# One address distance between weights and x in each product, 22 distances in the feed-forward pairs

## The chip, the core and the metric

The kernel runs on one core of a Trainium2 chip. The metric is the device time of one execution in microseconds, the median of several runs. Five engines work side by side and meet through semaphores: TensorE (PE, with its weight loads as PEld) multiplies, VectorE (DVE), ScalarE (ACT) and GpSimd (POOL) do everything elementwise, SyncE (SP) issues the DMAs that bring weights from HBM. Operands lie in SBUF, 128 partitions side by side; an address below is the byte offset within a partition. Products are accumulated in PSUM.

## What is computed

Two layers of a sequence model over 256 tokens behind 16 learned ones (272 rows of 1024 features). A layer has three mixers (retention, a gated linear recurrence, differential attention), whose inputs all come from one large projection, and a convolutional feed-forward part:

```python
def mixer(hn, w_in, w_branch, w_out, lb, lam_p, subln_g, lambda_init, valid, pos):
    proj = (hn @ w_in).astype(F32)
    ...
    y_b = jnp.einsum('blnc,ncd->blnd', branches, w_branch.astype(F32))
    gates = jax.nn.sigmoid(mg.reshape(b, l, N_BRANCH, D_MODEL))
    y = jnp.sum(gates * y_b, axis=2)
    return y.astype(hn.dtype) @ w_out

def conv_ffn(hn, w_ffn_in, conv_w, conv_b, w_ffn_out, valid):
    u = jnp.where(valid[None, :, None], hn @ w_ffn_in, 0.0)
    ...
    gate, val = jnp.split(c, 2, axis=-1)
    return (jax.nn.silu(gate) * val) @ w_ffn_out
```

with `h = h + mixer(rms_norm(h))` and `h = h + conv_ffn(rms_norm(h))` in each layer and a last norm. Nearly all arithmetic is in the five kinds of weight products (`w_in`, `w_branch`, `w_out`, `w_ffn_in`, `w_ffn_out`), all in float32.

## The kernel before

Activations lie transposed: features on the partitions, the 272 tokens along the row. Weights stream from HBM in **tiles** of 128 x 128, eight tiles to a **chunk** (512 KB). A chunk lands in `wraw`; ScalarE rounds it to a high part `whi` and VectorE subtracts to get the low part `wlo`. Each operand has such a high and a low part too. So every tile is three matmuls (lines 868 to 870): high weights by high x, high weights by low x, low weights by high x. In the profile the three lines give the beat of TensorE's stream, one beat of three for each tile.

The products are written in **pairs** of output tiles, named by matrix: `hq`, `hf` and so on to `m2` (the 52 pairs of `w_in`, table `BASE`), `b0` to `b2`, `wo`, `fi` (22 pairs, the feed-forward input) and `fo` (4 pairs, the feed-forward output). `ORDER` (line 58) lists them, `_turns` (line 87) the tiles of each pair: for the k tiles of the contraction in turn, the two outputs f. A pair of `w_in` or `fi` has 16 tiles (8 k tiles by 2), a pair of `fo` 44. In pair 3 of `fo` of layer 0 all k come first for one output, then for the other.

In the last layer only the tokens from `T0` = 14 on are needed by most products ("short" ones, 258 words instead of 272); those listed in `FULL` still take all 272. `fo` of the last layer is turned round (weights moving, 512 words, lines 1378 to 1380).

**Places.** The x of the projections and of `fi` lies in six tiles `xs` (line 725): high and low parts of k tiles 0 to 3 and 4 to 7, and a second set for 0 to 3. Each holds four k tiles of 272 words (1088 bytes, which is 64 more than a multiple of 256). `_places` (line 125) gives each weight tile its place in `whi` and `wlo`: it starts at a wanted offset modulo `LINE` = 256 bytes, and adds 64 bytes for every k tile (modulo four), so that within a pair the distance from x to the weights stays the same. In the program as it is allocated the tiles of x begin on a multiple of 256 bytes and all weight buffers 64 bytes behind one. That makes a distance of 64 bytes for full products and of 104 for short ones (96 + 64, less the 56 bytes of `T0`). Products whose operand lies in a **slot** (`b0` to `b2`, `wo`, `fo`) get 64 more, since the slots begin at 64; they have the same distances of 64 and 104. Where the wanted place is `None` (pair 3 of `fo` in layer 0, and `fo` in the last layer) the tiles lie back to back, 512 bytes each.

`_runs` (line 150) merges tiles of a chunk at equal steps, so that one instruction of ScalarE and one of VectorE write a chunk with its gaps.

Slots are 14 buffers of 4 x 272 words (`SLOTS`, line 38) that are used in rotation for heads, attention, operands of later products and the like. The order of all instructions is set before the run by `_Plan.order` from estimated costs and due times, with the number of buffers of each kind as a limit; engines then wait for each other by semaphores only. SP holds one queue: the loads of the weights and of a few constants, in that planned order.

Of the kernel before, what the change touches and what calls it, by code (L numbers as in the profile page):

```python
# [12 lines left out]
F32R = mybir.dt.float32r  # L13
# [6 lines left out]
P = 128  # L20
# [3 lines left out]
T = META + SEQ  # L24
D = 1024
KD = D // P
# [8 lines left out]
TAIL = T - 2 * P  # L35
BANK = 512
CHUNK_TILES = 8
SLOTS = 14
LEAD = 6.0
MARGIN = 12.0  # L40
EARLY = 12.0
# [6 lines left out]
BASE = {"rq": 0, "rk": 4, "rv": 8, "rg": 16, "hq": 24, "hf": 32, "hi": 40, "hg": 48,  # L48
        "dq": 56, "dk": 64, "dv": 72, "m0": 80, "m1": 88, "m2": 96}
# [37 lines left out]
def _turns(li):  # L87

    pairs = [x for x in ORDER if x[0][0] not in MARKS]
    if li == DEPTH - 1:
        pairs = [x for x in pairs if x[0] != "fo"]
    groups = [[x] for x in pairs]
    if li == 0:
        groups[:2] = [pairs[:2]]
    turned = [[x] for n in (BASE, ("fi",)) for x in [x for x in pairs if x[0] in n][DEFER - 1 : DEFER]]
    out = []
    for group in groups:  # L100
        if group == [("fo", 3)]:
            out.append([("fo", 3, k, f) for f in range(2) for k in range(FK)])
        else:
            nk = _ktiles(group[0][0])
            out.append([x + (k, f) for k in range(nk // 2) for x in group for f in range(2)])
            out[-1] += [x + (k, f) for x in group for k in range(nk // 2, nk) for f in range(2)]
            if group in turned:
                out[-1] = out[-1][nk:] + out[-1][:nk]
    if li == DEPTH - 1:
        out.append([("fo", j, k, f) for k in range(FK) for j in range(KD // 2) for f in range(2)])  # L110
    return out
# [5 lines left out]
LINE = 256  # L117
APART = (0, 96)
BLOCK = 64
ROOM = CHUNK_TILES * P + 2 * LINE // 4  # L120
T0 = META - 2
FULL = ("rk", "rv", "hf", "hi", "dk", "dv")


def _places(depth=DEPTH):

    wants = []
    for li in range(depth):  # L130
        for name, j, k, _ in sum(_turns(li), []):
            if name == "fo" and (li == DEPTH - 1 or j == 3):
                wants.append(None)
                continue
            short = li == DEPTH - 1 and name not in FULL
            wants.append(APART[short] + BLOCK * (name[0] == "b" or name in ("wo", "fo")) + 64 * (k % 4))
    out = []
    for c in range(0, len(wants), CHUNK_TILES):
        at, places = 0, []
        for want in wants[c : c + CHUNK_TILES]:  # L140
            if want is not None:
                at += (want // 4 - at) % (LINE // 4)
            places.append(at)
            at += P
        assert at <= ROOM
        out.append(places)
    return out
# [410 lines left out]
class _Weights:  # L558
# [3 lines left out]
    def __init__(self, plan, pool, w, act, dve, sp):  # L562
        self.plan, self.pool, self.w = plan, pool, w
        self.act, self.dve, self.sp = act, dve, sp
        self.used = 0
        self.places = _places()
# [37 lines left out]
def build(tc, a, depth=DEPTH, probe=None):  # L604
    with ExitStack() as ctx:
        plan = _Plan(tc)
        _trace(ctx, tc, plan, a, depth, probe or {})
        plan.issue()
    return plan


def _trace(ctx, tc, plan, a, depth, probe):
# [9 lines left out]
    wp = ctx.enter_context(tc.tile_pool(name="wp", bufs=3))  # L622
    sp = ctx.enter_context(tc.tile_pool(name="sp", bufs=SLOTS))
    gp = ctx.enter_context(tc.tile_pool(name="gp", bufs=3))
# [7 lines left out]
    def new(pool_, shape, dt, tag, bufs, name):  # L632
        serial[0] += 1
        return plan.tile(pool_, shape, dt, tag, bufs, f"{name}_{serial[0]}")

    def fixed(shape, name, dt=F32):
        return new(cp, shape, dt, name, 1, name)

    def slot(name, dt=F32):
        return new(sp, [P, 4 * T], dt, "slot", SLOTS, name)  # L640

# [80 lines left out]
    fmap = fixed([P, DEPTH], "fmap")  # L722
    fixed([P, KD], "step")

    xs = [[fixed([P, KD // 2, T], f"x{n}{i}", F32R) for n in "hl"] for i in range(3)]

    def x_tile(k, folded):
        return tuple(t[:, k % 4, :] for t in xs[1 if k >= 4 else 2 if folded else 0])
# [116 lines left out]
    def products(xs, name, j, t0=0):  # L845

        if name in BASE or name == "fi":
            norm.next()
        if ahead:
            return ahead.pop()  # L850
        tiles = turns.pop(0)
        main = lambda: new(mp, [P, 2, 512], F32, "main", 2, "main")[:, :, t0:T]
        ps = {i: main() for i in sorted({x[1] for x in tiles})}
        to = {x: ps[x[0]][:, x[1], :] for x in {x[1::2] for x in tiles}}
        if (name, j) == ("fo", 3):

            to[j, 1] = main()[:, 1, :]
        cost = 3 * ((T - t0) / 2400 + 0.003)
        left = dict.fromkeys(to, _ktiles(name))
        for _, i, k, f in tiles:  # L860
            hi, lo = (x[:, t0:] for x in xs(k))
            begun = left[i, f] < _ktiles(name)
            left[i, f] -= 1
            plan.key = clock[0]
            wh, wl = weights.next()

            def run(o=to[i, f], wh=wh, wl=wl, hi=hi, lo=lo, first=not begun, last=left[i, f] == 0):
                nc.tensor.matmul(o, wh, hi, start=first, stop=False)  # L868
                nc.tensor.matmul(o, wh, lo, start=False, stop=False)  # L869
                nc.tensor.matmul(o, wl, hi, start=False, stop=last)  # L870

            plan.main.append(plan.add("pe", run, cost, [to[i, f]], [wh, wl, hi, lo]))
            clock[0] += cost
        plan.key = clock[0] - 1.0
        if (name, j) == ("fo", 3):
            return [to[j, f] for f in range(2)]
        ahead.extend(ps[i] for i in ps if i != j)
        return ps[j]
# [64 lines left out]
    for li in range(depth):  # L943
# [458 lines left out]
        for name, j in ORDER:  # L1402
# [18 lines left out]
            elif name[0] == "*":  # L1421
                plan.key = clock[0] - MARGIN
                n = name[1:]
# [10 lines left out]
            if name in BASE:  # L1434
                lo = 0 if name in FULL else t0
                ps = products(lambda k: x_tile(k, norm.folded), name, j, lo)
# [30 lines left out]
                elif name in ("hi", "dv"):  # L1467
                    n = name[0] + "v"
# [109 lines left out]
```

## Time and profile before

| | |
|---|---|
| median of three runs | 1329.39 us (1329.1 to 1330.91) |
| span of the profiled execution, first to last instruction | 1327.6 us |
| difference, around the span | 1.8 us |
| matmuls in the three lines of the weight products | 9168 |
| DMA | 219.07 MB, 165 GB/s in the mean |

The profile shows one execution. Its page gives each engine's busy share, and the views of the trace give groups of instructions by line, waits, and instructions in order of time. In the view by line a row reads: line, engine, operation, output<-inputs, count; then the shortest, median and longest duration in ns and the start of the first and of the last one in us. Matmuls overlap each other in the records, so a matmul's duration is no measure of the pace; the distance from start to start is.

The waits of the whole program by the waits view, longest first (who waited, for whom, total us, times, longest):

```profile
POOL tails L553 <- ACT vsrc L553: 369.7, 23, 57.2
POOL y L553 <- ACT rstd L553: 316.7, 4, 188.3
DVE wlo L553 <- ACT whi L553: 199.8, 175, 4.7
ACT whi L553 <- PE main L869: 162.2, 134, 3.1
```

These are waits of engines that have time to spare: POOL has little to do, ScalarE waits for a weight buffer that TensorE gives back, and VectorE for ScalarE's cast.

### The profile page before, as it was taken

To read this page: it belongs to the slowest core of one execution; us is meant where nothing else is said; L and a number is where in the kernel's file an instruction comes from. 1 tells how busy PE (TensorE), PEld (TensorE's weight loads), DVE (VectorE), ACT (ScalarE), POOL (GpSimd) and SP (SyncE) were. 2 spreads that over 40 slices of the span, in tenths; PEclk is the share of its full clock that TensorE was granted. 3 is DMA by queue.
4 is the path that set the end of the run, shared out by engine and by line. 5 is a ranking of instruction groups with operands and counts; after the bars stand their busy time and mean duration, and the time that the engine had idled before them with its cause. 6 is when DMAs were issued, how large, how long until landed. Compare 5 with 4: busy or idle time off the path is not lost.

```text
span 1327.6 us, 28926 instructions
## 1 busy us (share of the span) xinstructions
PE 1317.0 (99%) x11862; PEld 1288.8 (97%) x11862; DVE 962.7 (73%) x1630; ACT 816.7 (62%) x1374; POOL 83.6 (6%) x161
## 2 busy tenths in 40 slices
PE   9999999999999999999999999999999999999998
PEld 9999999999999999999999999999999999999986
DVE  7675777697586789886574757776985867898753
ACT  6747454756676567666456474557565775767643
POOL 5000000001010020000030000000011100200000
PEclk9999999999999999999999999999999999999999
DMA  7644543443534545555555445444445446465653
GB/s 272 195 146 155 170 150 128 143 143 129 188 131 158 177 157 176 187 168 186 175 175 181 155 159 161 160 140 143 143 149 175 142 162 199 135 208 189 201 182 109
DMA packets 60755, 219.07 MB, mean 165 GB/s; under 512 B 6864, under 2 KB 6992, under 8 KB 60624
## 3 DMA queue, kind: packets, MB, share of 16 engines
q1 hardware_dynamic: 60336, 216.71, 49.1%
q8 instruction: 93, 1.52, 0.5%
q10 hardware_dynamic: 288, 0.52, 0.1%
q14 instruction: 38, 0.31, 0.1%
HBM read 216.16 MB, written 1.05 MB: 164 GB/s over the span
## 4 chain that ended last, share of the span: by engine, by line
PE 95%; DVE 3%; issue 1%; DMA 0%; ACT 0%; SPq 0%; DVEq 0%
PE main L868 28%; PE main L870 27%; PE main L869 27%; PE fo L1380 2%; PE fo L1378 2%; PE fo L1379 2%; PE lev L1059 1%; DVE two_b L553 1%; PE ds L1243 1%; PE ms L553 1%; PE do L553 1%; DVE wlo L553 1%; PE ro L553 1%; PE ho L553 1%; PE vt L553 1%
## 5 line engine op out<-in xcount | busy, mean ns | idle before, releaser
L868 PE MATMUL main<-xh,whi 128*128 128x272 f32 (+1 forms) x2368 | 693.2, 293 | 0.2 <-ACT whi L553 0.2
L870 PE MATMUL main<-xh,wlo 128*128 128x272 f32 (+1 forms) x2368 | 680.5, 287 | 0.8 <-DVE wlo L553 0.7
L869 PE MATMUL main<-xl,whi 128*128 128x272 f32 (+1 forms) x2368 | 671.6, 284 | 1.6 <-DVE xl L553 1.5
L553 DVE TENSOR_TENSOR wlo<-wraw,whi 128x1024 fp32r<-128x1024 f32 (+1 forms) x408 | 497.1, 1223 | 200.9 <-ACT whi L553 199.8
L553 ACT ACTIVATE whi<-wraw 128x1024 fp32r<-128x1024 f32 (+1 forms) x408 | 426.6, 1048 | 229.5 <-PE main L869 162.2
L869 PEld LDWEIGHTS main<-xl,whi 128*128 128x128 f32 x2368 | 448.9, 190 | 2.5 <-DVE xl L553 2.1
L868 PEld LDWEIGHTS main<-xh,whi 128*128 128x128 f32 x2368 | 445.6, 188 | 2.5 <-issue 0.7
L870 PEld LDWEIGHTS main<-xh,wlo 128*128 128x128 f32 x2368 | 444.6, 188 | 2.2 <-DVE wlo L553 2.1
L553 DVE SCALAR_TENSOR_TENSOR two_b<-main,small,two_b 128x256 f32<-128x256 f32 (+2 forms) x144 | 65.3, 488 | 29.1 <-ACT two_b L553 27.4
L553 POOL TENSOR_TENSOR y<-h,rstd 128x272 f32<-128x272 f32 x32 | 34.6, 1114 | 316.7 <-ACT rstd L553 316.7
L553 ACT ACTIVATE two_b<-main,small 128x272 f32<-128x272 f32 (+1 forms) x72 | 37.3, 567 | 26.8 <-PE main L870 26.6
L870 PE MATMUL main<-ghi,wlo 128*128 128x272 f32 x176 | 51.0, 290 | 0.0
L868 PE MATMUL main<-ghi,whi 128*128 128x272 f32 x176 | 50.9, 289 | 0.0
L869 PE MATMUL main<-glo,whi 128*128 128x272 f32 x176 | 50.2, 285 | 0.0
L553 ACT ACTIVATE vsrc<-main 128x544 f32<-128x544 f32 x24 | 15.0, 626 | 39.4 <-PE main L870 39.2
L868 PE MATMUL main<-b0hi,whi 128*128 128x272 f32 (+1 forms) x128 | 38.1, 298 | 0.0
L868 PE MATMUL main<-b1hi,whi 128*128 128x272 f32 (+1 forms) x128 | 38.1, 298 | 0.0
L870 PE MATMUL main<-yhi,wlo 128*128 128x272 f32 (+1 forms) x128 | 36.7, 286 | 0.0
L870 PE MATMUL main<-b2hi,wlo 128*128 128x272 f32 (+1 forms) x128 | 36.6, 286 | 0.0
L870 PE MATMUL main<-b1hi,wlo 128*128 128x272 f32 (+1 forms) x128 | 36.6, 286 | 0.0
L870 PE MATMUL main<-b0hi,wlo 128*128 128x272 f32 (+1 forms) x128 | 36.6, 286 | 0.0
L868 PE MATMUL main<-yhi,whi 128*128 128x272 f32 (+1 forms) x128 | 36.5, 285 | 0.0
(244 smaller groups left out, 1936.4 us busy)
## 6 DMA issues: line engine op xcount, KB each, us to landing
wraw<-in_w SPq DMA_DIRECT2D x402, 512.0 KB, 3.4
h<-in_h SPq DMA_DIRECT2D x4, 272.0 KB, 5.2
dec<-in_dec SPq DMA_DIRECT2D x2, 544.0 KB, 5.4
wraw<-in_w SPq DMA_DIRECT2D x4, 256.0 KB, 4.6
const<-in_const SPq DMA_DIRECT2D x1, 937.0 KB, 6.1
gain<-in_gl SPq DMA_DIRECT2D x1, 512.0 KB, 6.1
out<-y ACTq DMA_DIRECT2D x2, 256.0 KB, 2.8
out<-y SPq DMA_DIRECT2D x2, 256.0 KB, 2.7
```

What stands on the lines that cost most here:

```text
L553: self.plan.add(self.name, lambda: f(*args, **kw), cost, outs, ins, args[2] if method == "activation" else None)
L868: nc.tensor.matmul(o, wh, hi, start=first, stop=False)
L869: nc.tensor.matmul(o, wh, lo, start=False, stop=False)
L870: nc.tensor.matmul(o, wl, hi, start=False, stop=last)
L1059: nc.tensor.matmul(o, keys, x, start=True, stop=True)
L1243: nc.tensor.matmul(ss[m][:, at : at + nk], q[half, hd, q0 : q0 + P], k[half, hd, :nk], start=True, stop=True)
L1378: nc.tensor.matmul(o, gh, wh, start=False, stop=False)
L1379: nc.tensor.matmul(o, gl, wh, start=False, stop=False)
L1380: nc.tensor.matmul(o, gh, wl, start=False, stop=end)
```

## The change

```diff
-SLOTS = 14
+SLOTS = 13
...
+SPREAD = [16 * i for i in range(16)] + [8 + 40 * i for i in range(6)]
+WIDE = 320
...
             short = li == DEPTH - 1 and name not in FULL
+            if name in BASE or name == "fi":
+                wants.append((SPREAD[j] + 4 * T0 * short if name == "fi" else APART[short]) % LINE)
+                continue
             wants.append(APART[short] + BLOCK * (name[0] == "b" or name in ("wo", "fo")) + 64 * (k % 4))
...
-    xs = [[fixed([P, KD // 2, T], f"x{n}{i}", F32R) for n in "hl"] for i in range(3)]
+    xs = [[fixed([P, KD // 2, WIDE], f"x{n}{i}", F32R)[:, :, :T] for n in "hl"] for i in range(3)]
```

- Each k tile of x takes 320 words (1280 bytes, five times 256) instead of 272, of which the same 272 are used. All k tiles of x so begin at the same offset modulo 256.
- The weights of the 52 pairs of `w_in` are all put at `APART`, without the 64 bytes for each k tile. Their distance from x is 64 for full and 104 for short products, as before; what goes is that the offset of both moves with k.
- The weights of `fi` pair j are put at `SPREAD[j]` (with 56 bytes for the short ones of the last layer, to make up for `T0`): sixteen multiples of 16, then 8, 48, 88, 128, 168, 208. With the 64 bytes at which the weight buffers begin the distances are 64 + `SPREAD[j]` modulo 256, the same list in both layers.
- The wider x takes 4608 bytes more of each partition; one slot of 4352 bytes is given up. The addresses of slots and weight buffers stay 64 past a multiple of 256.

The built program has the same instructions in the same order on all five engines. What differs in them, beside addresses, is the shape of the casts: where tiles stood at steps of 64 bytes, a chunk was written as four runs of 256 words; now one run of 1024 does it. On ScalarE, in the middle of the feed-forward input of layer 0, before (`whi` is the rounded chunk, `two_b` the convolution, `ghi` the high part of the gated product):

```order
L553 ACTIVATE whi_1031<-wraw_1030 128x4x256
L553 ACTIVATE ghi_1015<-two_b_1017 128x272
L553 ACTIVATE two_b_1025<-main_1018,small_76 128x272 x2
L553 ACTIVATE whi_1036<-wraw_1035 128x4x256
L553 ACTIVATE two_b_1025<-two_b_1025 128x272
L553 ACTIVATE whi_1039<-wraw_1038 128x4x256
```

and with the change:

```order
L558 ACTIVATE whi_1031<-wraw_1030 128x1024
L558 ACTIVATE ghi_1015<-two_b_1017 128x272
L558 ACTIVATE two_b_1025<-main_1018,small_76 128x272 x2
L558 ACTIVATE whi_1036<-wraw_1035 128x1024
L558 ACTIVATE two_b_1025<-two_b_1025 128x272
L558 ACTIVATE whi_1039<-wraw_1038 128x1024
```

Nothing has moved; the cast of each chunk is one run. VectorE's subtraction changes in the same way. Since a slot now comes round after 13 uses, a dozen of the waits on semaphores differ (nine on POOL, two on VectorE, one on SP).

## Prediction

> **What bounds the kernel now.** I read the page's first two parts, then the waits of TensorE (PE), then single stretches by line and in order of time. The first rows of the page:
>
> ```profile
> span 1327.6 us, 28926 instructions
> PE 1317.0 (99%) x11862; PEld 1288.8 (97%) x11862; DVE 962.7 (73%) x1630; ACT 816.7 (62%) x1374; POOL 83.6 (6%) x161
> PEclk9999999999999999999999999999999999999999
> ```
>
> PE has work in 99% of the span and the granted clock never falls. Everything that PE waited for by the waits view is small; the two longest rows are
>
> ```profile
> PE main L869 <- DVE xl L553: 1.5, 1, 1.5
> PE warm L553 <- POOL ones_d L553: 1.0, 1, 1.0
> ```
>
> So no wait sets the time; the pace does at which one matmul follows another. Over fourteen feed-forward pairs of layer 0 (8 to 21), over a stretch of thirteen pairs of layer 1, and over the last branch product of layer 1, the instructions of line 868 (the first of the three matmuls of every weight tile) read
>
> ```profile
> L868 PE MATMUL main<-xh,whi x224: 287/288/289, 525.4 to 608.8; 128*128 128x272 f32 x112
> L868 PE MATMUL main<-xh,whi x208: 278/283/284, 1178.0 to 1252.4; 128*128 128x258 f32 x104
> L868 PE MATMUL main<-b2hi,whi x64: 278/284/287, 1084.1 to 1106.5; 128*128 128x258 f32 x64
> ```
>
> First start to last start over the count less one is the time of a tile (three matmuls): 83.4 / 223 = 374.0 ns with 272 words, 74.4 / 207 = 359.4 ns with 258 words, and 22.4 / 63 = 355.6 ns for the same 258 words in the branch product. The last two have the same address distance (104 bytes) and differ by 1%: a distance alone does not fix a pace; how the stream came into step counts too.
>
> Why a distance could matter is seen in order of time:
>
> ```profile
> 150.07 0.29 PE L868 MATMUL main<-xh,whi 128*128 128x272 f32 x1
> 150.08 0.19 PEld L869 LDWEIGHTS main<-xl,whi 128*128 128x128 f32 x1
> 150.20 0.28 PE L869 MATMUL main<-xl,whi 128*128 128x272 f32 x1
> 150.21 0.19 PEld L870 LDWEIGHTS main<-xh,wlo 128*128 128x128 f32 x1
> ```
>
> The load for the next matmul starts 0.01 us after the current matmul does: weights and x are read from SBUF at the same moment, each time with the same offset between the two addresses.
>
> **What a distance is worth.** One place of the trace shows it with all else alike. In layer 0, feed-forward output pairs 0 to 2 have weights at 64 bytes from their operand; pair 3 has its tiles back to back, so that its distance goes through 0, 64, 128 and 192. Same width, same order of three matmuls:
>
> ```profile
> L868 PE MATMUL main<-ghi,whi x132: 286/289/290, 609.2 to 658.2; 128*128 128x272 f32 x132
> L868 PE MATMUL main<-ghi,whi x28: 285/289/292, 658.6 to 668.8; 128*128 128x272 f32 x28
> ```
>
> 49.0 / 131 = 374.0 ns against 10.2 / 27 = 377.8 ns: 3.8 ns more a tile, 1%. The first four tiles of pair 3 have distances 128, 64, 0, 192:
>
> ```profile
> 658.57 0.29 PE L868 MATMUL main<-ghi,whi 128*128 128x272 f32 x1
> ...
> 658.95 0.29 PE L868 MATMUL main<-ghi,whi 128*128 128x272 f32 x1
> ...
> 659.32 0.29 PE L868 MATMUL main<-ghi,whi 128*128 128x272 f32 x1
> 659.45 0.29 PE L869 MATMUL main<-glo,whi 128*128 128x272 f32 x1
> 659.58 0.29 PE L870 MATMUL main<-ghi,wlo 128*128 128x272 f32 x1
> 659.70 0.29 PE L868 MATMUL main<-ghi,whi 128*128 128x272 f32 x1
> ```
>
> 0.38, 0.37 and 0.38 us: 64 is the quickest of the three, and the whole spread is some 3%. Single starts there lie 0.12 to 0.13 us apart.
>
> A rule of the Trainium skill speaks against any effect: "TensorE: Matmul & The Clock Gate", section "Step-by-step: what each phase is for", gives TensorE two independent SBUF read ports, so that loading the next weights takes no read bandwidth from the running matmul. By it all distances cost alike and every term below would be 0, which is the last of the rivals. The two rows of line 868 above disagree, by 1%.
>
> **The change part by part.** *Feed-forward input pairs.* Two layers of 22 pairs of 16 tiles, 352 tiles a layer. x now starts every k tile on a 256-byte boundary, the weights of pair j lie 64 + SPREAD[j] behind it (the 64 is where the weight buffers begin), so 64 gives way to all multiples of 16 and a few of 8. In layer 0 I take the mean of pair 3's four distances for the mean over the 22: +3.8 x 352 = +1.3 us. In layer 1 the distance given up is 104 at 359.4 ns a tile; no row there has another distance, so I take the same +3.8, again +1.3 us. Ends for each layer: below, every tile as the quickest rows (0.37 us in layer 0, 355.6 ns in layer 1), about -1.4 us; above, each matmul at the slowest printed step, 0.13 us, 390 ns a tile, +16 x 352 = +5.6 us in layer 0 and taken alike in layer 1. Eighteen of the 22 places have never run here, hence the wide upper end; I choose near the measured four since every step seen lies within 0.13 us.
>
> *All products of x (52 pairs a layer).* Before, x moved 64 bytes with every k and the weights with it, so the load that crosses to the next k stood 64 bytes further off for one matmul in six; now it does not. Two tiles in turn show it in both widths:
>
> ```profile
> 540.35 0.29 PE L868 MATMUL main<-xh,whi 128*128 128x272 f32 x1
> ...
> 540.72 0.29 PE L868 MATMUL main<-xh,whi 128*128 128x272 f32 x1
> ...
> 541.10 0.29 PE L868 MATMUL main<-xh,whi 128*128 128x272 f32 x1
> ```
> ```profile
> 1094.08 0.28 PE L868 MATMUL main<-b2hi,whi 128*128 128x258 f32 x1
> ...
> 1094.44 0.28 PE L868 MATMUL main<-b2hi,whi 128*128 128x258 f32 x1
> ...
> 1094.79 0.28 PE L868 MATMUL main<-b2hi,whi 128*128 128x258 f32 x1
> ```
>
> 0.37 then 0.38; 0.36 then 0.35. The mixer's pairs keep their 64 and 104, so this is all that changes for them: 74 pairs of 272 words (1184 tiles) and 30 of 258 (480 tiles). Ends: all tiles like the shorter (370 and 350 ns) -4 x 1184 - 9.4 x 480 = -9.2 us; all like the longer (380 and 360 ns) +6 x 1184 + 0.6 x 480 = +7.4 us. Which it is the trace cannot say, for a longer tile may only return what the one before gained. I take 0 for the wide ones, since 374.0 lies midway, and for the narrow ones the step from 359.4 to 355.6, -3.8 x 480 = -1.8 us, halved because much of the mixer runs between other PE work: -0.9 us.
>
> *Casts.* ScalarE and VectorE now write each chunk of eight tiles as one run instead of four. Rows for the two forms, from the feed-forward stretch and from the contiguous chunks of the end:
>
> ```profile
> L553 DVE TENSOR_TENSOR wlo<-wraw,whi 128x1024 fp32r<-128x1024 f32 x30 | 36.5, 1218 | 0.7 <-ACT whi L553 0.7
> L553 DVE TENSOR_TENSOR wlo<-wraw,whi 128x1024 fp32r<-128x1024 f32 x20 | 24.5, 1225 | 25.1 <-ACT whi L553 25.1
> ```
>
> 1218 and 1225 ns: no difference, and PE waited for nothing in the first of these stretches. 0 us.
>
> *13 slots.* The order on all five engines stays; a dozen waits change. The two new ones on VectorE, before a write of dq, are for a POOL copy made 105 us earlier, and the load of dec, which stands in SP's queue ahead of weight loads, now waits for a memset of hq, 100 us earlier:
>
> ```profile
> 837.67 0.35 POOL L553 COPY tw<-rk 128x128 f32<-128x128 f32 x1
> 942.62 0.68 DVE L553 TENSOR_TENSOR dq<-main,const 128x516 f32<-128x516 f32 x1
> 748.94 0.15 POOL L553 MEMSET hq<- 128x56 f32 x1
> L553 SPq DMA_DIRECT2D dec<-in_dec x2: 383/404/424, 184.8 to 849.2; - x2
> ```
>
> 0 us. If such a cover were gone, the VectorE work behind dq and the weight loads behind dec would stop, and PE with them; 100 us of slack makes that remote.
>
> Sum: 1.3 + 1.3 - 0.9 = +1.7 us on the profiled span, 1329.3 us. The span lies 1.8 us under the median of the runs (1329.39), so the time is 1329.4 + 1.7 = **1331.1 us**.
>
> **The rivals.** *Costly distances.* The untried places, most of them not multiples of 64, collide at nearly every read, and one pair of two runs at 0.13 us a matmul. For: 0 and 128 already cost more than 64, and in layer 1 the weights come to addresses that are 8 past a multiple of 16, where none was. Against: no four-distance mean is far off. Price: 352 tiles (half of both layers) x 16 = 5.6, the other half at +3.8 is 1.3, less 0.9: +6.0 us, 1335.4. It decides from a mean of 383 ns a tile in layer 0.
>
> The page "SBUF — State Buffer", section "Specifications (TRN2)" of the Trainium skill gives SBUF 16-byte lines and a penalty for each access that crosses to a new one; a weight row that begins 8 bytes into a line touches 33 lines for 32. What that costs no row here shows for weights.
>
> *The even stream is quicker (the other side).* Without the jump of 64 the x products fall into the shorter step, 371 ns for the wide and 353 for the narrow tiles. For: alternate tiles of both streams already have it. Against: pair 3's one tile of 64 without a jump gave 0.37 as well, and its neighbours took the gain back. Price: -3 x 1184 = -3.6, -6.4 x 480 = -3.1, with +2.6 for the feed-forward pairs: -4.1 us, 1325.3. It decides from 372 ns a tile in the wide mixer pairs.
>
> *Distance does nothing* outside pair 3, whose back-to-back tiles are slow for another reason: all terms 0, 1329.4.
>
> **How the numbers follow.** Forecast 0.41, costly distances 0.36, quicker stream 0.18, nothing 0.05. About 0.2% (2.7 us) is what a measurement of this kernel can tell from no change; the forecast and nothing lie inside it, the other two outside: faster 0.18, same 0.46, slower 0.36. The range goes from 1325 (the quicker stream) to 1338 (costly distances with some pairs worse than half at 0.13); it leaves out the far ends of -12 and +18 us.
>
> **What would show it.** In the changed profile: the 22 feed-forward pairs of layer 0, 16 tiles each, should no longer read alike but spread between 370 and 385 ns a tile, mean near 378, with the pair at 64 still near 374; layer 1 near 363. The mixer's wide tiles should stay at 374. PE's waits should stay at a few us, and the branch, wo and fo products unchanged. The forecast is wrong if single pairs exceed 390 ns, if the mixer's tiles move by more than 2 ns, or if a wait of PE's of some us stands where there was none.

## The result, and the profile after

The changed kernel takes 1326.36 us (median of 11 runs, 1325.87 to 1327.05) against 1329.39 us before (11 runs on the same chip, 1328.23 to 1330.91): ratio 0.9975, 95% interval 0.9967 to 0.9984. The forecast was 1331.1 us. The time lies inside the stated range and just outside the 0.2% band, on the faster side. The rival that "the even stream is quicker" had 1325.3 us.

The page of the changed kernel, first lines:

```profile
span 1324.6 us, 28929 instructions
PE 1314.0 (99%) x11862; PEld 1285.7 (97%) x11862; DVE 962.4 (73%) x1630; ACT 816.4 (62%) x1374; POOL 83.2 (6%) x161
```

The span fell by 3.0 us and PE's busy time by the same 3.0 us, while the other engines did the same work. The waits of PE in the changed kernel, the two longest:

```profile
PE main L874 <- DVE xl L558: 1.3, 1, 1.3
PE warm L558 <- POOL ones_d L558: 1.0, 1, 1.0
```

All that PE waited for in this view adds up to 4.1 us in both traces, so the gain is no wait that went: the pace changed. The view by line gives it, as in the prediction: first to last start over the count less one. The first matmul of each tile (now line 873) in six undisturbed wide pairs of the mixer, in fi pairs 8 to 21 of layer 0 (from within pair 8), and in fi pairs 8 to 20 of layer 1; after them the last branch product of layer 1, which the change does not touch. The first row shows the same 96 tiles of the mixer in the kernel before:

```profile
L868 PE MATMUL main<-xh,whi x96: 287/288/289, 37.9 to 73.5; 128*128 128x272 f32 x96
L873 PE MATMUL main<-xh,whi x96: 285/286/288, 38.4 to 73.5; 128*128 128x272 f32 x96
L873 PE MATMUL main<-xh,whi x214: 284/288/295, 526.9 to 607.2; 128*128 128x272 f32 x107
L873 PE MATMUL main<-xh,whi x211: 277/282/287, 1173.8 to 1249.3; 128*128 128x258 f32 x106
L873 PE MATMUL main<-b2hi,whi x64: 278/283/289, 1080.6 to 1103.2; 128*128 128x258 f32 x64
```

35.1 / 95 = 370 ns for the mixer's wide tiles (35.6 / 95 = 374.7 before; 374.0 in hg pairs 0 to 3 by the starts in ns), 80.3 / 213 = 377.0 for the feed-forward tiles of layer 0 (374.0 before), 75.5 / 210 = 359.5 for those of layer 1 (359.4 before). The branch product moved from 355.6 to 22.6 / 63 = 358.7 with the same addresses modulo 256 and the same code.

Where the 3 us went, from the start of the first matmul of each pair in the two traces:

| stretch | before us | after us | difference |
|---|---|---|---|
| up to the first product | 6.1 | 5.6 | -0.5 |
| 52 wide mixer pairs, layer 0 | 360.0 | 358.2 | -1.8 |
| 22 wide mixer pairs, layer 1 | 150.9 | 150.0 | -0.9 |
| 30 narrow mixer pairs, layer 1 | 199.7 | 198.6 | -1.1 |
| 22 feed-forward input pairs, layer 0 | 133.4 | 134.1 | +0.7 |
| the same, layer 1 (pairs 0 to 20) | 123.0 | 123.0 | +0.1 |
| branch, wo and fo products | 279.7 | 280.1 | +0.4 |

The feed-forward pairs lost a little, the mixer gained more. The first row hardly belongs to the change: in the runs below, it lies anywhere between 5.6 and 6.9 us. Each of the 22 distances, in ns a tile (three times the mean from start to start within the pair; intervals over 145 ns, which are interruptions, left out):

| distance | 0 | 16 | 32 | 48 | 64 | 72 | 80 | 96 | 112 | 128 | 144 |
|---|---|---|---|---|---|---|---|---|---|---|---|
| layer 0 | 376 | 375 | 380 | 380 | 370 | 371 | 380 | 371 | 380 | 380 | 371 |
| layer 1 | 360 | 360 | 360 | 360 | 361 | 360 | 353 | 360 | 361, 360 | 357, then 420 | 363 |

| distance | 152 | 160 | 176 | 192 | 208 | 224 | 232 | 240 |
|---|---|---|---|---|---|---|---|---|
| layer 0 | 383 | 376 | 376 | 380 | 377 | 377 | 374 | 375 |
| layer 1 | 360 | 350 | 363 | 360, 359 | 355 | 360 | 356 | 360 |

Two pairs each have 16, 112 and 192; they agree to 1 ns. The means are 376.6 and 360.1 ns. The highest of the wide tiles is 383 ns: none comes near the 390 that the prediction's upper end allowed. In the narrow pair at 128 the pace changed at an interruption half way, from 357 ns a tile to 2.1 / 5 = 420 ns, without any wait after it:

```profile
L873 PE MATMUL main<-xh,whi x6: 306/306/306, 1155.1 to 1157.2; 128*128 128x258 f32 x6
```

### The profile page after: what moved, and what is told of

Same layout as the page of the kernel before. It is cut to its first block, busy times and chain, and to the rows that moved or that the text cites. A ratio compares the mean times of both kernels' runs of the same rounds, so it can differ in the third digit from the quotient of the medians.

```text
span 1324.6 us, 28929 instructions
## 1 busy us (share of the span) xinstructions
PE 1314.0 (99%) x11862; PEld 1285.7 (97%) x11862; DVE 962.4 (73%) x1630; ACT 816.4 (62%) x1374; POOL 83.2 (6%) x161
## 4 chain that ended last, share of the span: by engine, by line
PE 95%; DVE 3%; ACT 1%; issue 0%; DMA 0%; SPq 0%; DVEq 0%
PE main L873 28%; PE main L875 27%; PE main L874 27%; PE fo L1383 2%; PE fo L1385 2%; PE fo L1384 2%; PE lev L1064 1%; DVE two_b L558 1%; PE ds L1248 1%; PE ms L558 1%; PE do L558 1%; PE ro L558 1%; PE ho L558 1%; PE vt L558 1%; DVE wlo L558 1%; PE s L558 0%
## 5 line engine op out<-in xcount | busy, mean ns | idle before, releaser
L873 PE MATMUL main<-b2hi,whi 128*128 128x272 f32 (+1 forms) x128 | 36.5, 285 | 0.0
```

## The experiments

Theory: TensorE's stream is quicker when every weight load stands at the same offset from the x being read, and in the mixer the change does just that; the 22 distances give part of it back. Rivals: the spread itself, the slots, or the 256-byte boundary on which x now begins. All times below are beside runs of the kernel before on the same chip.

**One distance for all products of x.**

```diff
 # changed kernel
-                wants.append((SPREAD[j] + 4 * T0 * short if name == "fi" else APART[short]) % LINE)
+                wants.append(APART[short])
```

> The changed kernel with the feed-forward pairs at the mixer's distances, 64 and 104, in place of the 22. Theory (the steady offset gains, the 22 distances give part of it back): the feed-forward tiles fall to the mixer's pace of the changed kernel, 370 ns in layer 0 and 353.5 ns in layer 1, that is about 2.4 and 2.0 us less: 1322.0 us. Rival (the 22 distances are themselves the gain, or cost nothing): 1326.4 us or more.

Measured: 1324.64 us (6 runs, 1322.46 to 1325.26), ratio to before 0.9969 (0.9956 to 0.9981). Feed-forward tiles in both layers of this kernel:

```profile
L873 PE MATMUL main<-xh,whi x217: 285/285/288, 524.9 to 604.8; 128*128 128x272 f32 x109
L873 PE MATMUL main<-xh,whi x207: 278/278/278, 1171.9 to 1244.7; 128*128 128x258 f32 x104
```

79.9 / 216 = 369.9 ns and 72.8 / 206 = 353.4 ns, as the theory had it. The profiled run took 1322.46 us, the others up to 2.8 us more; the repetition below shows why.

The casts change their form wherever the step goes, so they are a rival for this gain. The same trace answers it, because the casts run ahead of PE. While wo pairs 2 and 3 of layer 0 run, whose weights still step, the chunks that are cast from 464.0 us on are those of `fi`, each in one run. While fi pairs 20 and 21 run, which do not step, the chunks from 596.4 us on are those of `fo`, each in four:

```profile
L873 PE MATMUL main<-yhi,whi x32: 287/288/289, 460.9 to 472.5; 128*128 128x272 f32 x32
L873 PE MATMUL main<-xh,whi x32: 285/286/288, 593.3 to 604.8; 128*128 128x272 f32 x32
```

11.6 / 31 = 374 ns and 11.5 / 31 = 371 ns: each stream keeps its own pace whatever casts run beside it.

**13 slots alone.**

```diff
 # kernel before
-SLOTS = 14
+SLOTS = 13
```

> The kernel before with 13 slots and nothing else. Theory: 1329.4 us, the wide feed-forward tiles at 374 ns. Rival (the moved slots and waits give the gain): 1326.4 us.

Measured: 1329.32 us, ratio 1.0001 (0.9992 to 1.0009). The slots and the dozen changed waits do nothing.

**The 22 distances alone, with the step of 64 bytes.**

```diff
 # kernel before
             short = li == DEPTH - 1 and name not in FULL
+            if name == "fi":
+                wants.append((SPREAD[j] + 4 * T0 * short + 64 * (k % 4)) % LINE)
+                continue
```

> The kernel before (x at 272 words, weights moving 64 bytes with k) with the 22 distances for the feed-forward pairs and nothing else. Theory: the mixer stays at 374 and 359 ns a tile; the feed-forward pairs of layer 0 spread and are slower in the mean by 1 to 4 ns a tile: 1329.5 to 1331.5 us. Rival (spreading the distances gains by itself): under 1328 us.

Measured: 1330.32 us, ratio 1.0012 (1.0003 to 1.0021). The feed-forward tiles of layer 0:

```profile
L872 PE MATMUL main<-xh,whi x226: 282/287/299, 524.7 to 609.4; 128*128 128x272 f32 x113
```

84.7 / 225 = 376.4 ns, 2.4 more than with one distance and the same step: the spread by itself loses. The mixer stayed as before (360.1 us for its wide pairs of layer 0).

Set beside the changed kernel, which has the same 22 distances without the step, this run shows something more. The stretch quoted gave 377.0 ns there, and over all 22 pairs of layer 0 the means are 376.3 ns with the step and 376.6 without. At 64 and 96 bytes the pair with the step is slower (374 against 370 ns, 376 against 371), at 80 and 112 it is quicker (376 against 380 ns, 377 against 380). So a step is no loss as such: without one, a distance runs at a pace of its own, good or bad, and 64 is one of the good ones.

**x 64 bytes past the boundary.**

```diff
 # changed kernel, one distance
-                wants.append(APART[short])
+                wants.append((APART[short] + 64) % LINE)
...
-    xs = [[fixed([P, KD // 2, WIDE], f"x{n}{i}", F32R)[:, :, :T] for n in "hl"] for i in range(3)]
+    xs = [[fixed([P, KD // 2, WIDE], f"x{n}{i}", F32R)[:, :, 16 : 16 + T] for n in "hl"] for i in range(3)]
```

> One distance for all products of x and no step with k, as in the kernel with one distance, but x begins 64 bytes past a 256-byte boundary and the weights move with it. Theory (only the offset between weights and x counts, and that it is steady): same as the kernel with one distance, 1322.0 us, 370 ns a wide tile. Rival (it is the boundary on which every k tile of x begins): wide tiles back at 374 ns, narrow at 359 ns, 1329 us.

Measured: 1325.69 us (9 runs, 1323.4 to 1326.71), ratio 0.9974 (0.9964 to 0.9983). Layer 0, then layer 1:

```profile
L873 PE MATMUL main<-xh,whi x216: 285/286/288, 525.1 to 604.6; 128*128 128x272 f32 x108
L873 PE MATMUL main<-xh,whi x207: 282/285/285, 1171.9 to 1246.7; 128*128 128x258 f32 x104
```

79.5 / 215 = 369.8 ns: for the wide tiles the boundary has no part in it. The narrow ones gave 74.8 / 206 = 363.1 ns, which neither theory had named: slower than with the step of 64 bytes (359.4), at the same distance of 104 that had just run at 353.4. This miss led to the next run.

**One distance once more.** The kernel of the first experiment again, on another chip.

> The kernel with one distance once more, on another occasion. Theory (the narrow stream has two rhythms at the same addresses, 353.4 and 363.3 ns a tile, and which one it falls into after an interruption can differ between executions): wide tiles at 370 as before; feed-forward of layer 1 at one of the two values, times between 1322 and 1326 us. Rival (the addresses alone set the rhythm): 353.4 ns again.

Measured: 1325.19 us (5 runs, 1322.82 to 1326.78), ratio 0.9962 (0.995 to 0.9975). In its profiled execution, fi pairs 1 to 4 of layer 1 (up to an interruption within pair 4) and fi pairs 8 to 20:

```profile
L873 PE MATMUL main<-xh,whi x50: 278/278/278, 1133.9 to 1151.2; 128*128 128x258 f32 x50
L873 PE MATMUL main<-xh,whi x213: 282/285/285, 1171.8 to 1248.8; 128*128 128x258 f32 x107
```

17.3 / 49 = 353 ns, then 77.0 / 212 = 363.2 ns: the same code, addresses and distance, 3% apart within one execution, and in the first profile of this kernel the second stretch ran at 353.4. Even the recorded duration of one matmul tells the two apart (278 against 285 ns). So the narrow stream at distance 104 has two rhythms, and it changes over at an interruption, here in pair 4. Over fi pairs 5 to 21 of layer 1 (272 tiles) the difference of 10 ns is 2.7 us, the size of the scatter between the runs of this kernel.

The kernel before, whose narrow stream steps, has two paces at 104 as well: by the method of the table, fi pairs 2 and 3 of layer 1 ran at 354.2 ns and pairs 6 to 20 at 359.0 in its one trace. So for the narrow tiles no step against a step is one pair of paces against another (353 and 363 against 354 and 359), and what they gained in the changed kernel (353 ns in hg pairs 0 to 3, 359 before) can't be put down to the missing step alone.

**The step at other sizes.** Three kernels keep 64 and 104 within a tile and let x and the weights step by another amount, so that the load that crosses to the next k stands elsewhere.

```diff
 # step 128
-WIDE = 320
+WIDE = 288
...
-                wants.append((SPREAD[j] + 4 * T0 * short if name == "fi" else APART[short]) % LINE)
+                wants.append((APART[short] + 128 * (k % 2)) % LINE)
```
```diff
 # step 80
+WIDE = 276
...
+                wants.append((APART[short] + 80 * (k % 4)) % LINE)
...
+    xs = [[fixed([P, 1152], f"x{n}{i}", F32R)[:, : KD // 2 * WIDE].rearrange("p (a t) -> p a t", t=WIDE)[:, :, :T] for n in "hl"] for i in range(3)]
```
```diff
 # step -64
-SLOTS = 13
+SLOTS = 12
...
-ROOM = CHUNK_TILES * P + 2 * LINE // 4
+ROOM = CHUNK_TILES * P + 3 * LINE // 4
...
+WIDE = 304
...
+                wants.append((APART[short] - 64 * (k % 4)) % LINE)
```

> x in k tiles of 288 words, so that the weights step by 128 bytes with k; distances 64 and 104 within a tile, 192 and 232 on the load that crosses to the next k, instead of 128 and 168 before. Theory (the load at the other offset costs, and what it costs is the pace of that offset): the wide tiles in pairs, about 373 to 374 ns in the mean, since 192 and 128 ran alike in layer 0 of the changed kernel: 1328 to 1330 us. Rival (any step is harmless, it was 128 and 168 alone that cost): 370 ns, 1324.6 us.

> x steps by 80 bytes with k and the weights with it, so that two crossing loads of three stand at 144 instead of 128 (the third, from k tile 3 to 4, at 80). In the changed kernel pairs of one distance ran at 371 ns a tile at 144, 380 at 80 and 128. Theory A (each load costs what its own offset costs, one load in six is a crossing one): wide feed-forward tiles of layer 0 at 370 to 371.5 ns. Theory B (any step between tiles breaks the quick rhythm, whatever the offset): 373 to 374 ns, as with 128 and 192.

> x steps back by 64 bytes with k and the weights with it (12 slots, 256 bytes more in each weight buffer); crossing loads stand at offset 0, where a pair of one distance ran at 376 ns a tile in the changed kernel. Theory A (own offset of each load): 371 ns for the wide feed-forward tiles of layer 0. Theory B (any step breaks the rhythm): 373 to 374 ns.

Measured: step 128, 1330.46 us, ratio 1.0009 (1.0000 to 1.0018); the other two were run once each (1335.54 and 1328.47 us beside 1329.99 before; in the first, two breaks of 3.5 us together inside the recurrence's small matmuls, of no cause that the profile shows, so that only its pace is used). Feed-forward tiles of layer 0 for steps of 128, 80 and -64:

```profile
L873 PE MATMUL main<-xh,whi x223: 286/287/291, 524.9 to 607.8; 128*128 128x272 f32 x112
```
```profile
L873 PE MATMUL main<-xh,whi x224: 283/287/291, 524.9 to 607.9; 128*128 128x272 f32 x112
```
```profile
L873 PE MATMUL main<-xh,whi x223: 287/288/290, 525.0 to 607.7; 128*128 128x272 f32 x112
```

82.9 / 222 = 373.4, 83.0 / 223 = 372.2 and 82.7 / 222 = 372.5 ns, beside 374.0 with the step of 64 and 369.9 without one. Theory A, a sum over the offsets of the single loads, gives 370 + 3 / 6 of the difference per matmul: 371.6, 370.6 and 371. (With the step of 80, three crossing loads of four stand at 144 and the fourth at 80, not two of three as the expectation counts.) All three are above it by 1.5 to 2 ns. Theory B (373 to 374) is nearer, though two of the three fall half a ns or more below it. At the distance of 64 any of these steps costs 2 to 4 ns a tile; its size adds little. The time with the step of 128 lies above the 1330 us of its theory because the narrow tiles, which the theory had left out, went to 365 ns a tile in fi pairs 6 to 20 of layer 1.

**A step after every tile.**

```diff
 # kernel before, SLOTS = 13, ROOM with 3 * LINE // 4
+            if group[0][0] in BASE or group[0][0] == "fi":
+                half = lambda ks: [x + (k, f) for x in group for f in range(2) for k in ks]
+                out[-1] = half(range(nk // 2)) + half(range(nk // 2, nk))
             if group in turned:
```

> The kernel before with 13 slots and the tiles of a pair in another order: four k for one output, then four for the other, so that every tile ends on the step to the next k, not every second. Theory (the step costs about 4 ns for a tile over its absence, in the mean of both): wide feed-forward tiles go up from 374 to 377 or 378 ns, the mirror image of the gain; in all 3 to 6 us more, 1332 to 1335 us, with another 2 us possible at the start, where x comes later than it is wanted. Rival (something else in the layout of x gained): 374 ns, unchanged.

Measured: 1359.73 us, ratio 1.0226 (1.0212 to 1.0240), far outside the expected 1332 to 1335. Of the 30 us that the span grew, 28 lie in the feed-forward pairs, and most of it is not the question's: in this order one output of a pair is complete and is read by ScalarE while the other half of the same PSUM tile is still being written, and PE waits:

```profile
PE main L871 <- ACT two_b L556: 21.2, 30, 1.0
```

The pace away from these waits answers the question. Some six wide mixer pairs:

```profile
L871 PE MATMUL main<-xh,whi x102: 287/288/291, 36.0 to 73.7; 128*128 128x272 f32 x102
```

37.7 / 101 = 373.3 ns: not 377 or 378, and not above the 374 of half as many steps. The feed-forward pairs of layer 0, which the expectation named, ran at 372.6 to 373.5 ns between their interruptions. So a price for each step is wrong too. At the distance of 64, what counts is whether the stream steps at all.

**Another distance for the narrow tiles.**

```diff
 # changed kernel, one distance
-                wants.append(APART[short])
+                wants.append(152 if short else 0)
```

> One distance for all products of x without the step, 64 for the wide ones and 160 for the narrow ones (the quickest of the 22 in layer 1 of the changed kernel, 350 ns a tile in pair 6). Theory (a distance has its own pace, and carries it to other pairs): feed-forward of layer 1 at 350 ns in all pairs, narrow mixer tiles near that where nothing disturbs them: 1320 to 1322.5 us. Rival (a stream of one distance has several rhythms, pair 6 happened to fall into a quick one): pairs at 350 beside pairs well above it, or all near 360, and a time like the kernel with 104, 1324.6 us, or over it.

Measured: **1320.65 us** (5 runs, 1320.23 to 1321.44), ratio to before 0.9933 (0.9920 to 0.9945), the quickest of all. Feed-forward of layer 1:

```profile
L873 PE MATMUL main<-xh,whi x215: 278/278/279, 1167.8 to 1242.7; 128*128 128x258 f32 x108
```

74.9 / 214 = 350.0 ns, the pace that pair 6 had shown in the changed kernel, now in all these pairs, and the undisturbed narrow mixer pairs have it as well (350 ns in hg pairs 0 to 3). No second rhythm showed, and the runs lie within 1.2 us of each other.

## Why the prediction was wrong

It forecast +1.7 us on the span; -3.0 was measured. Step by step:

- *PE's pace is the bound, no wait moves, 13 slots and the casts are free:* right. PE's waits are as before, and the kernel before with 13 slots alone gave 1.0001.
- *Feed-forward pairs of layer 0, +3.8 ns a tile:* near. The mean of the four distances in `fo` pair 3 was 377.8 ns; the 22 pairs ran at 377.0 in the stretch quoted. In time it came to +0.7 us instead of +1.3.
- *Feed-forward pairs of layer 1, +3.8 ns a tile:* mis-sized, +0.1 us for +1.3. The excess was carried over from layer 0, where the distance given up was the best of all. In layer 1 it was not: 104 with the step gave 359.4 ns, and the 22 distances without it gave 359.5 in the stretch quoted.
- *All products of x, 0 for the wide tiles and -0.9 us for the narrow ones:* here the forecast failed. The wide tiles went to 370 ns and gave -1.8 and -0.9 us, the narrow ones -1.1. The step that fell is "I take 0 for the wide ones, since 374.0 lies midway": the longer and the shorter tile in turn were read as one borrowing from the other. Without the step both run at the shorter one's 370 ns, as the rival on the other side had it; its bound of -4 ns a tile, which stood in the text, was the answer for undisturbed pairs. In time that bound would have been -4.7 us; -2.7 was measured, since pairs that are often interrupted gained less. The term for the narrow tiles came out by luck: the 359.4 and the 355.6 from which it is taken are the two paces of one stream with the step, and no measure of what the step costs.
- *The even stream is quicker,* at 1325.3 us, came near, but partly by errors that cancel: its terms were -3.6, -3.1 and +2.6 us, measured were -2.7, -1.1 and +0.8.
- *Distance does nothing* is refuted for the pace: weights at 64 and at 152 bytes from x differ by 13 ns a tile in layer 0, with the same code. So what the prediction drew from the rule of the Trainium skill on two independent read ports ("TensorE: Matmul & The Clock Gate", section "Step-by-step: what each phase is for"), that all distances cost alike, does not hold here. The penalty for crossing 16-byte lines, which the Trainium skill gives on the page "SBUF — State Buffer", section "Specifications (TRN2)", does not show: of the 22 narrow pairs only those at 72, 152 and 232 have weights on a multiple of 16, and their 360, 360 and 356 ns lie among the rest.

Its own signs of being wrong showed: the mixer's wide tiles moved by 4 ns where 2 was the limit, and the branch product moved by 3. Some small readings were off as well, without bearing on the result: with 192 twice in the list, 17 and not 18 of the 22 places had never run; the far upper end adds up to +18.6 us; and pair 3 of `fo`, called alike in all else, also takes its tiles in another order and steps after each.

Shown by runs: the wide tiles' gain came from the steady offset of the x products at 64 bytes (370 ns in every run without a step, 372 to 374 in every run with one), and the 22 distances cost 2.4 ns a tile with the step and 7 without it in layer 0 (376.4 against 374.0, 377.0 against 369.9). Shown as well: the boundary of x, the slots and the casts have no part for the wide tiles. Not shown: that a steady stream is quicker at any distance (over the 22 it is not), and why it is at 64. A price for each offset gives too little, and a price for each step too much; the weights read, the x read and the two rhythms of the narrow stream look like one mechanism of streams that lock into each other, but no run here separates it. The branch product's +3 ns a tile, with untouched addresses, is a change between the two paces of the narrow stream with the step: pairs 1 to 3 of it ran at 354.2 ns before and at 359.0 after, the two values that fi pairs of layer 1 showed before. It ran at 354 with 13 slots alone and with the 22 distances alone, and at 359 in all the other runs, so it is no scatter; what sets it is open. The products that read slots (branch, wo, fo) still step; slots of 320 words in the number that they need have no room beside the rest, and that was not tried.

## What to carry to other kernels

When matmuls follow each other without a wait, the start-to-start time of a long undisturbed stretch is the quantity to watch, and here it moved by 1 to 4% with where stationary and moving operands lie. Pad the rows so that every weight load of a stream stands at the same offset from its operand, then try offsets in one profiled run, one for each of many like pairs, and give the best to all. The padding pays only together with a good offset: over the 22 distances here, the wide streams had the same mean with and without a step. Where two tiles alternate in length, do not take their mean for the pace of the steady case.

## What the runs showed of the hardware

- The offset between weights and moving operand modulo 256 bytes changes the pace of a stream that keeps it: 370 to 383 ns a tile of three 272-word matmuls, 350 to 363 for 258 words, and 420 in half a pair at 128. The best differs by width: 64 for the wide (72, 96 and 144 within about 1 ns of it), 160 for the narrow ones.
- At one offset the narrow stream ran at 353 or at 363 ns a tile, in one execution and from one execution to another, and changed over at an interruption. With a step of 64 bytes it ran at 354 or at 359.
- At 64 bytes, with one matmul of three or of six loading at another offset, the wide tiles took 372 to 374 ns; with none, 370. At 80 bytes it was the other way round: 376 with the step of 64, 380 with none.
